# Samples' scores in short-lived banks, seven page slots, and half of w_out split during heads 2 to 5

## The chip, the cores and the metric

One core of one Trainium2 chip runs the whole kernel. The metric is the device time of one execution in microseconds; the time before is the median of three runs. A core has five engines with a queue each: TensorE (PE; its weight loads are PEld), VectorE (DVE), ScalarE (ACT), GpSimd (POOL) and SyncE (SP, which issues most DMAs here). Each engine takes its instructions in the order in which they were written for it.

## The reference

One layer of a decoder on 1024 prompt tokens and 8 samples of 4 tokens, width 1024, all in fp32:

- `z = LN(x) @ w_in`, cut into q, k, v, forget logits and the state-space input u
- attention: 8 heads of 64, `softmax(q k^T / 8 + c_q - c_k) v` with c the running sum of the forget logs; the prompt is causal over itself; each sample attends to 512 cached positions (4 pages of 128 rows, found by a page table) and its own 4
- the state-space mixer, then a gated unit: `y * sigmoid(y @ w_glu + b_glu)`
- `h1 = LN1(alpha h + concat(att, ssm) @ w_out)`, and after it a feed-forward layer, a gated embedding and LN2

## The kernel before, in words

Every matmul of fp32 precision is made of three in a faster format: an operand is split into a rounded part (hi, made by ScalarE) and a residual (lo, a subtraction); `split` is the helper, and hi*hi + hi*lo + lo*hi are summed. So a weight costs a load of its raw values, a ScalarE cast and a VectorE subtraction before PE can use it.

The change lies in the stage between about 290 and 545 us. Work there has three strands. **Heads.** For head h, `loads(h)` brings queries and keys into four tiles (eight DMAs, 1.6 MB), `weights(h)` makes the scores and exponentials of eight blocks of 128 queries, and `values(h)` does twelve steps: PE transposes the exponentials (tile tw), ScalarE copies them out (pe), VectorE rounds them (ph), GpSimd takes the residual (pl), PE multiplies both with the values (po; L909, L910). After step 4 and step 12 a half of the output is summed (oh) and sent to `mixd`. Values come with 0.25 MB a head, outputs leave with 0.25 MB. Scores run four blocks ahead of values. **The gated unit** (`glu`) reads y (`load_y`), splits it into slots u, multiplies, applies tanh, and writes `mixd` rows 512 and up (mo). **Samples** (`sample`) work in two halves of four samples: 16 key pages of 128x512 (0.26 MB each) are transposed on PE (tk) and copied out by ScalarE and VectorE in turn, 16 small matmuls after every fourth page give the scores (ssm, L990); then softmax, then five value steps of eight matmuls each (L1035), the first four with four value pages each. Pages go through six slots; `page()` issues the next load.

Gated unit and samples are generators in a queue `bg`, traced in between by `fill(t)`: each step has a price, and fill lets steps be traced until their prices reach the budget. The prices sum to 22.2 (gated unit) and 44.6 (samples). The budgets before the last scores sum to 61: 20 before head 0, 0.35 a step in heads 0 to 3, 0.6 after. A planner then orders each engine's instructions by a timeline of its own; `tc.issue_after(newest(SP))` forbids it to put a DMA ahead of SP's newest one at that point.

**After the heads** `load_wo` loads and splits w_out, 128 rows at a time: rows 4 to 7 (for the mixer's half of the input) into a pool opened when the query tiles are closed, rows 0 to 3 after the heads' pool is closed. `half(i, 4)` and `half(i, 0)` multiply a tile of 128 tokens of `mixd` with the two halves of w_out; `load_mx` loads that tile. The first two tiles' mixer halves run as `ssm` beside the last eight steps of head 7. PSUM has eight banks: three for scores (s), two for transposes (t), one for po (o) and two (f) that gated unit and samples share.

Of the kernel before, what the change touches and what calls it, by code (L numbers as in the profile page):

```python
# [8 lines left out]
F32 = mybir.dt.float32  # L9
F32R = mybir.dt.float32r  # L10
# [59 lines left out]
def fox_s5_step(tc, a, o):  # L70
# [764 lines left out]
    msk = aq_.tile([128, 512], F32, name="msk", bufs=1)  # L835
    G.memset(msk[:, 0:384], 0.0)
    G.tensor_copy(msk[:, 384:512], cst[:, TRI:TRI + 128])
    ins_, vs_, rows = {}, {}, {}

    def loads(h):  # L840
        hs_ = slice(h * 64, h * 64 + 64)
        qa = aq_.tile([128, T], F32R, tag="qa", name="qa")
        qb = aq_.tile([68, T], F32R, tag="qb", name="qb")
        ka = aq_.tile([128, T], F32R, tag="ka", name="ka")
        kb = aq_.tile([68, T], F32R, tag="kb", name="kb")
# [41 lines left out]
    def values(h):  # L887
# [5 lines left out]
        for u in range(2):  # L893
# [35 lines left out]


    def sample(bp):
        def page():
            t = bp.tile([128, AW], F32, tag="pg", name="pg", bufs=6)
            i, z = todo.pop(0)
            if z == "cache_k":
                pvs[i] = SY.value_load(idr[0:1, i:i + 1], min_val=0, max_val=a["cache_k"].shape[1] - 1)
            pv = pvs[i] if z == "cache_k" else pvs.pop(i)
            SY.dma_start(out=t, in_=a[z][0][bass.DynSlice(pv, 1)].rearrange("n t h d -> (n t) (h d)"))
            pages.append(t)
# [20 lines left out]
        for h in range(H):  # L960
# [5 lines left out]
                for g in range(4) for b4 in range(4)]  # L966
        for _ in range(6 - 1):
            page()
        yield 0.0
        for half in range(2):  # L970
            sel = cst[0:64, SEL + half * 128:SEL + half * 128 + 128]
            ps = bank("ssm", "f")
            PE.matmul(ps, lhsT=sel, rhs=nc_[:, 0:512], start=True, stop=False, skip_group_check=True)
            for g in range(4):
                kT = slot(2 + g % 2, F32)[:, 0:2048].rearrange("p (a b c) -> p a b c", a=4, b=4)
                for b4 in range(4):
                    kp = pages.pop(0)
                    if todo:
                        page()
                    t = bank("tk", "f").rearrange("p (k c) -> p k c", k=4)  # L980
                    for hp_ in range(4):
                        PE.transpose(t[:, hp_], kp[:, hp_ * 128:hp_ * 128 + 128], ident)
                    if b4 % 2:
                        V.tensor_copy(kT[:, b4], t)
                    else:
                        S.copy(kT[:, b4], t)
                    yield 0.45
                for hp_ in range(4):
                    for b4 in reversed(range(4)):
                        PE.matmul(ps[b4 * 32:b4 * 32 + 32, g * 128:g * 128 + 128], lhsT=qbd[:, half * 4 + b4, hp_],  # L990
                                  rhs=kT[:, b4, hp_], start=False, stop=(g == 3 and hp_ == 3),
                                  tile_position=(0, b4 * 32), skip_group_check=True)
                yield 0.95
            pn = bank("ssn", "f")[:, 0:8]
# [46 lines left out]
            om = bp.tile([128, AW], F32, tag="om", name="om", bufs=1)  # L1041
# [12 lines left out]

    for n in range(2):
        gp.tile([128, NB], F32, tag="sg", name="sg", bufs=2)
    gp.tile([128, NT], F32, tag="mo", name="mo")

    def load_y(m):
        t = gp.tile([128, NB], F32, tag="yf", name="yf", bufs=4)  # L1060
        if m < 3:
# [7 lines left out]
    def glu():  # L1069
# [16 lines left out]
        for m in range(4):  # L1086
            hi, lo = (x[:, :, m % 2 * 128:m % 2 * 128 + 128] for x in w[m // 2])
            sg = gp.tile([128, NB], F32, tag="sg", name="sg", bufs=2)
            yf = ys[m]
# [15 lines left out]
            ts(V, sg, sg, 0.5, MUL, 0.5, ADD)  # L1105
            mo = gp.tile([128, NT], F32, tag="mo", name="mo")
            yv = yf.rearrange("p (l c) -> p c l", l=L)
# [3 lines left out]
            SY.dma_start(out=mixd[AW + 128 * m:AW + 128 * m + 128], in_=mo)  # L1111
        gctx.close()

# [11 lines left out]
    bp = pool("smp", 2, stack=smctx)  # L1125
    ap_ = pool("att", 2, stack=actx)
    bg += [glu(), sample(bp)]
    lsum = ap_.tile([128, H, 12], F32, name="lsum", bufs=1)
    fill(1e-3)
    vload(0)  # L1130
    for i in range(4):
        steps(1)
        fill(5)
        if i == 1:
            loads(1)
    for h in range(H - 1):
# [18 lines left out]
    wo = {}  # L1155

    def load_wo(k, p, q, e=V):
        hi, lo = (p.tile([128, D], F32R, name=f"wo{n}{k}") for n in "hl")
        raw = q.tile([128, D], F32, tag="raw" if q is wp else "z", name="rawo", bufs=2 if q is wp else 3)
        SY.dma_start(out=raw, in_=a["w_out"][0][k * 128:(k + 1) * 128])  # L1160
        split(raw, hi, lo, e)
        wo[k] = hi, lo

    for k in range(4, 8):
        load_wo(k, woa, wp, V)
    mixv = mixd.rearrange("(k p) t -> p k t", p=128)
    dv = "p (c n) -> p c n"
    mxs, pss, order = {}, {}, [0, 1, 2, 3, 4, 5, 8, 6, 7]

    def load_mx(i):  # L1170
        mx = wp.tile([128, KD, 128], F32, tag="raw", name="mx", bufs=2)
        t0, r = tiles[i]
        SY.dma_start(out=mx[:, 4:8, :r], in_=mixv[:, 4:8, t0:t0 + r])
        return mx, [wp.tile([128, KD, 128], F32R, tag=t, name=t, bufs=2) for t in ("whi", "wlo")]

    def half(i, k0):
        t0, r = tiles[i]
        if k0:
            mxs[i] = load_mx(i)
            pss[i] = [bank("pso", t) for t in ("ss", "so")[order.index(i) % 2]]  # L1180
# [55 lines left out]
    for k in range(4):  # L1236
        load_wo(k, wop, op, V)
        next(ssm, None)
        fill(.5)
# [5 lines left out]

    ub = {(kh, 0): [h1p.tile([128, 4, HN], F32R, name=f"u{n}{kh}") for n in "hl"] for kh in range(2)}
    pend = []
# [520 lines left out]
```

## Time and profile before

| | before |
|---|---|
| median of 3 runs | 1450.24 us (1448.77 to 1460.35) |
| profiled execution | 1455.53 us, span 1453.8 us |
| PE busy | 1367.5 us, 94% |
| PE weight loads | 1267.7 us, 87% |
| VectorE | 981.4 us, 68% |
| ScalarE | 635.3 us, 44% |
| GpSimd | 676.2 us, 47% |
| mean granted clock of PE | 0.973 of full speed |

The profile shows one execution. Busy time counts instructions alone, and a busy PE at the lower clock counts like one at full speed. Windows give, for a stretch, the busy time of each engine, the granted clock and what the DMA engines did. The list of waits names what an engine's idle time ended on. A line of a helper (L82 for every addition or product of two tiles, L157 for the cast of `split`) stands for many places, so tiles tell more than lines. SP's rows show when a DMA was issued, not when it landed.

### The profile page before, as it was taken

The numbers are of one execution on the slowest core, as the hardware profiler recorded it, in microseconds if no ns is written. First come the engines' busy times: TensorE is split into PE (matmuls) and PEld (weight loads), VectorE is DVE, ScalarE is ACT, GpSimd is POOL, SyncE is SP. The second block draws the span as 40 slices with busy tenths as digits, with TensorE's granted clock in tenths as the row PEclk, the third lists the DMA queues.
The fourth block names the chain that finished last, engine by engine and source line by source line (L and its number), as shares of the span: only waits on it lengthen the run. The fifth ranks groups of instructions, "written<-read, shape, count | busy, mean of one in ns | idle before, by whom it ended". The sixth has DMA issues, their size and how long they took to land. (4 is left out here: it accounts for less than half of the span.)

```text
span 1453.8 us, 26634 instructions
## 1 busy us (share of the span) xinstructions
PE 1367.5 (94%) x10045; PEld 1267.7 (87%) x10045; DVE 981.4 (68%) x1579; ACT 635.3 (44%) x1188; POOL 676.2 (47%) x639
## 2 busy tenths in 40 slices
PE   6997999978979789999999999999999999999896
PEld 5887899877857558789999999999999999999796
DVE  8549599747977836568846555554555888888567
ACT  4422444446766624443325445454466344434212
POOL 4313012026656600028845443344347787777845
PEclk8999999989999989999999999999999999999898
DMA  7564255596876573323234444434467344556922
GB/s 280 175 131 109 77 152 137 159 250 180 204 183 170 140 224 108 91 66 93 78 104 128 147 162 163 132 128 149 149 227 260 115 128 162 163 163 171 181 67 102
DMA packets 209193, 218.38 MB, mean 150 GB/s; under 512 B 43977, under 2 KB 166473, under 8 KB 209065
## 3 DMA queue, kind: packets, MB, share of 16 engines
q1 hardware_dynamic: 197288, 178.02, 42.8%
q0 software_dynamic: 11776, 38.67, 8.3%
q8 instruction: 79, 1.29, 0.4%
q14 instruction: 50, 0.40, 0.1%
HBM read 143.59 MB, written 66.55 MB: 145 GB/s over the span
## 5 line engine op out<-in xcount | busy, mean ns | idle before, releaser
L1408 PE MATMUL pd<-x,a 128*128 128x264 f32 x1344 | 173.9, 289 | 10.0 <-ACT a L157 3.8
L1408 PEld LDWEIGHTS pd<-x,a 128*128 128x128 f32 x1344 | 169.4, 192 | 11.9 <-POOL a L82 4.2
L82 DVE TENSOR_TENSOR pacc<-pd,pacc 128x528 f32<-128x528 f32 x180 | 122.0, 701 | 66.1 <-PE pd L1408 60.4
L157 ACT CAST a<-s 128x256 fp32r<-128x256 f32 (+1 forms) x176 | 82.2, 485 | 180.4 <-PE pd L1408 75.1
L82 DVE TENSOR_TENSOR wlo<-raw,whi 128x1024 fp32r<-128x1024 f32 x68 | 103.8, 1527 | 46.1 <-ACT whi L157 33.8
L82 POOL TENSOR_TENSOR pl<-pe,ph 128x512 fp32r<-128x512 f32 (+1 forms) x96 | 104.6, 1100 | 61.7 <-DVE ph L905 35.6
L1408 PE MATMUL pb<-th,a 128*128 128x264 f32 x768 | 132.3, 284 | 0.0
L82 POOL TENSOR_TENSOR a<-s,a 128x256 fp32r<-128x256 f32 x112 | 105.8, 1002 | 55.3 <-ACT a L157 55.2
L82 POOL TENSOR_TENSOR s<-raw 128x256 f32<-128x256 f32 (+1 forms) x72 | 77.9, 1132 | 88.2 <-DVE a L82 65.9
L1408 PE MATMUL pd<-x,whi 128*128 128x264 f32 x672 | 109.1, 284 | 0.6 <-DVE pacc L82 0.6
L1408 PEld LDWEIGHTS pb<-th,a 128*128 128x128 f32 x768 | 109.2, 189 | 0.0
L82 DVE TENSOR_TENSOR x<-x 128x1056 fp32r<-128x1056 f32 (+2 forms) x68 | 95.3, 1433 | 7.2 <-ACT x L1429 6.3
L183 PE MATMUL mmc<-hhi,whi 128*128 128x352 f32 x288 | 94.7, 329 | 0.0
L183 PE MATMUL mmc<-hhi,wlo 128*128 128x352 f32 x288 | 94.4, 328 | 0.0
L1408 PEld LDWEIGHTS pd<-x,whi 128*128 128x128 f32 x672 | 93.4, 188 | 0.8 <-DVE pacc L82 0.8
L183 PE MATMUL mmc<-hlo,whi 128*128 128x352 f32 x288 | 93.8, 326 | 0.0
L82 POOL TENSOR_TENSOR rs<-rs,mh 128x1 f32<-128x1 f32 (+1 forms) x27 | 19.5, 731 | 158.4 <-DVE rs L86 156.1
L82 DVE TENSOR_TENSOR a<-s,a 128x512 fp32r<-128x512 f32 x64 | 47.5, 746 | 47.1 <-ACT a L157 42.8
L157 ACT CAST whi<-raw 128x1024 fp32r<-128x1024 f32 x48 | 50.5, 1052 | 63.4 <-PE pa L1408 27.0
L1408 PE MATMUL pb<-tl,a 128*128 128x264 f32 x384 | 78.1, 285 | 0.0
L882 ACT ACTIVATE row<-ss,nm 128x384 f32<-128x384 f32 (+4 forms) x96 | 55.6, 585 | 34.3 <-DVE nm L878 33.1
L905 DVE CAST ph<-pe 128x512 fp32r<-128x512 f32 (+1 forms) x96 | 61.2, 650 | 10.5 <-PE po L909 4.6
(470 smaller groups left out, 3948.8 us busy)
## 6 DMA issues: line engine op xcount, KB each, us to landing
x<-gd SPq DMA_DIRECT2D x53, 528.0 KB
raw<-in_w_up_dram SPq DMA_DIRECT2D x32, 512.0 KB
raw<-in_w_down_dram SPq DMA_DIRECT2D x120, 128.0 KB
gd<-e POOLq DMA_DIRECT2D x14, 1056.0 KB, 7.4
gd<-c POOLq DMA_DIRECT2D x14, 792.0 KB, 5.4
pg<-in_cache_k_dram SPq DMA_DIRECT2D x32, 256.0 KB
pg<-in_cache_v_dram SPq DMA_DIRECT2D x32, 256.0 KB
pacc<-pacc POOLq DMA_DIRECT2D x24, 264.0 KB, 6.6
```

The source lines that it names most:

```text
L82: e.tensor_tensor(out, x, y, op=op)
L157: S.copy(hi, x)
L183: PE.matmul(out, lhsT=wt[:, k], rhs=xt[:, k, c0:c0 + n], start=(k == 0 and i == 0), stop=(k == nk - 1 and i == 2))
L882: S.activation(out=pr_[:, c * n:(c + 1) * n], in_=ps, func=AF.Exp, scale=-1.0, bias=nm[:, i:i + 1], accum_out=lsum[:, h, i + 4 * c:i + 4 * ...
L905: V.tensor_copy(ph, pe)
L1408: PE.matmul(ps[:, p, :PC], lhsT=wt[:, k], rhs=xt[:, k, p * PC:(p + 1) * PC], start=(start and k == 0 and j == 0), stop=(k == n - 1 and j = ...
```

## The change

A head's queries and keys now live in two tiles of 128x2112 each instead of four of 128x1024; there are four such tiles for two heads, and later they hold the projection's result (`ub`), which before had a pool of its own opened after the heads. The gated unit's tiles become eight fixed slots g0 to g7, and w_out rows 4 to 7 (hi and lo) take the same slots later; these rows are loaded and split at the start of heads 2, 3, 4 and 5, behind SP's newest DMA, and the first two mix tiles are loaded at head 6. A sample half's scores are made in four banks, one for every four pages, each copied to SBUF (p) at once. Pages have seven slots; om uses one of them. The last page of a half's value phase is issued one step later. Budgets are 0.5 a step in heads 0 to 3 and 0.7 after, 72 before the last scores. The mask, rl and rlt move to other tiles, and oh has one slot instead of two.

```diff
@@ -824 @@
-    qctx, actx, h1bctx, h1ctx, smctx, gctx = (ExitStack() for _ in range(6))
+    actx, h1bctx, h1ctx, smctx, woctx = (ExitStack() for _ in range(5))
     h1x = pool("h1x", stack=h1ctx, side="right")
-    aq_ = pool("attq", 2, stack=qctx, side="right")
-    gp = pool("glu", stack=gctx, side="right")
+    h1p = pool("h1", stack=h1ctx, side="right")
+    gp = pool("glu", stack=woctx, side="right")
+    def hslot(j):
+        return h1p.tile([128, 4 * HN], F32R, tag=f"h{j}", name=f"h{j}")
+    def gslot(j, shape, d=F32):
+        return gp.tile(shape, d, tag=f"g{j}", name=f"g{j}")
+    for j in range(8):
+        gslot(j, [128, L * CB if j < 6 else NT if j == 6 else D])
...
     def loads(h):
-        qa = aq_.tile([128, T], F32R, tag="qa", name="qa")
...
+        qt, kt = (hslot(h % 2 * 2 + j) for j in range(2))
+        qa, qb, ka, kb = qt[:, 0:T], qt[0:68, T:2 * T], kt[:, 0:T], kt[0:68, T:2 * T]
@@ -911 @@
-            oh = ap_.tile([64, 512], F32, tag="oh", name="oh", bufs=2)
+            oh = ap_.tile([64, 512], F32, tag="oh", name="oh", bufs=1)
@@ -928 @@
+    NPG = 7
     def sample(bp):
         def page():
-            t = bp.tile([128, AW], F32, tag="pg", name="pg", bufs=6)
+            t = bp.tile([128, AW], F32, tag="pg", name="pg", bufs=NPG)
@@ -964 @@
-        for _ in range(6 - 1):
+        for _ in range(NPG - 1):
             page()
...
-            ps = bank("ssm", "f")
-            PE.matmul(ps, lhsT=sel, rhs=nc_[:, 0:512], start=True, stop=False, skip_group_check=True)
@@ -985 @@
+                gs_ = slice(g * 128, g * 128 + 128)
+                ps = bank("ssm", "f")[:, 0:128]
+                PE.matmul(ps, lhsT=sel, rhs=nc_[:, gs_], start=True, stop=False, skip_group_check=True)
                 for hp_ in range(4):
                     for b4 in reversed(range(4)):
-                        PE.matmul(ps[b4 * 32:b4 * 32 + 32, g * 128:g * 128 + 128], lhsT=qbd[:, half * 4 + b4, hp_],
+                        PE.matmul(ps[b4 * 32:b4 * 32 + 32], lhsT=qbd[:, half * 4 + b4, hp_],
...
+                V.tensor_copy(p[:, gs_], ps)
@@ -1006 @@
-            ts(V, p[:, 0:512], ps, cq1, ADD)
+            ts(V, p[:, 0:512], p[:, 0:512], cq1, ADD)
@@ -1034 @@
-                for _ in range(4):
+                if g == 3:
+                    om = bp.tile([128, AW], F32, tag="pg", name="om", bufs=NPG)
+                for _ in range((4, 4, 4, 3, 0)[g]):
                     if todo:
                         page()
...
+            if todo:
+                page()
@@ -1124 @@
+    msk = ap_.tile([128, 512], F32, name="msk", bufs=1)
...
+    def load_wo(k, q, e=V):
+        if k > 3:
+            hi, lo = (gslot(2 * k - 8 + j, [128, D], F32R) for j in range(2))
+        else:
+            hi, lo = (wop.tile([128, D], F32R, name=f"wo{n}{k}") for n in "hl")
+        raw = q.tile([128, D], F32, tag="raw" if q is wp else "z", name="rawo", bufs=2 if q is wp else 3)
+        with ExitStack() as st1:
+            if k > 3:
+                st1.enter_context(tc.issue_after(newest(mybir.EngineType.SP)))
+            SY.dma_start(out=raw, in_=a["w_out"][0][k * 128:(k + 1) * 128])
+        split(raw, hi, lo, e)
+        wo[k] = hi, lo
...
     for h in range(H - 1):
+        if 2 <= h < 6:
+            load_wo(h + 2, wp, V)
+        elif h == 6:
+            mxs.update((i, load_mx(i)) for i in range(2))
         for j, _ in enumerate(values(h)):
             if j < 4 or j % 2:
                 steps(1)
-            fill(.35 if h < 4 else .6)
+            fill(.5 if h < 4 else .7)
@@ -1146 @@
-        fill(.6)
+        fill(.7)
     steps(1)
-    qctx.close()
-    h1p = pool("h1", stack=h1ctx, side="right")
-    woctx = ExitStack()
-    woa = pool("woa", stack=woctx, side="right")
...
-    for k in range(4, 8):
-        load_wo(k, woa, wp, V)
@@ -1215 @@
-    rl = ap_.tile([128, H, 8], F32, name="rl", bufs=1)
+    rl = ap_.tile([128, 512], F32, tag="pe", name="rl", bufs=4)[:, 0:8 * H].rearrange("p (h i) -> p h i", h=H)
...
-    rlt = ap_.tile([64, 128], F32, name="rlt", bufs=1)
+    rlt = ap_.tile([128, 512], F32, tag="pe", name="rlt", bufs=4)[0:64, 0:128]
@@ -1243 @@
-    ub = {(kh, 0): [h1p.tile([128, 4, HN], F32R, name=f"u{n}{kh}") for n in "hl"] for kh in range(2)}
+    ub = {(kh, 0): [hslot(2 * kh + j).rearrange("p (k n) -> p k n", k=4) for j in range(2)] for kh in range(2)}
```

## Rows read from the trace of the kernel before

**Rows 1.** windows: stretch, length, busy us (count) PE PEld DVE ACT POOL, PEclk, DMA

```profile
300.00:314.00 14.00, 6.41 (x31) 5.05 (x29) 4.26 (x5) 5.25 (x7) 1.22 (x1) 0.77 1.08 224
...
364.00:403.00 39.00, 37.29 (x352) 31.64 (x351) 35.47 (x79) 30.67 (x84) 27.30 (x26) 1.00 0.89 206
...
416.00:442.00 26.00, 20.03 (x113) 11.73 (x112) 15.34 (x34) 12.66 (x36) 12.49 (x13) 0.87 0.85 227
...
453.00:489.00 36.00, 33.99 (x299) 28.64 (x297) 30.89 (x72) 28.18 (x77) 26.09 (x25) 1.00 0.56 138
...
489.00:518.00 29.00, 22.04 (x161) 15.81 (x162) 20.99 (x32) 13.71 (x27) 11.19 (x9) 0.88 0.54 157
...
518.00:544.00 26.00, 21.85 (x96) 14.07 (x95) 6.79 (x8) 4.19 (x4) 0.00 (x0) 0.87 0.85 263
...
544.00:590.00 46.00, 46.00 (x220) 37.61 (x219) 25.85 (x55) 19.09 (x40) 2.26 (x4) 1.00 0.36 98
```

**Rows 2.** the list of waits of PE, 290 to 600: us in total, times, longest

```profile
PE po L1035 <- DMA pg<-in_cache_v_dram: 5.7, 3, 3.2
...
PE ss L872 <- DMA kb<-kkd: 5.1, 1, 5.1
...
PE pso L1196 <- ACT woh L157: 4.1, 1, 4.1
...
PE tpp L1020 <- DVE u L86: 3.1, 1, 3.1
...
PE tk L982 <- ACT u L986: 0.7, 1, 0.7
...
PE tk L982 <- DVE u L984: 0.7, 3, 0.3
```

**Rows 3.** the timeline of SP, 280 to 600: start, length, issues of DMAs

```profile
284.14 0.33 SPq L1160 DMA_DIRECT2D rawo<-in_w_out_dram  x1
...
345.77 0.47 SPq L916 DMA_DIRECT2D mixd<-oh  x1
...
426.56 0.96 SPq L938 DMA_DIRECT2D pg<-in_cache_v_dram  x2
...
520.04 2.07 SPq L938 DMA_DIRECT2D pg<-in_cache_v_dram  x4
...
522.22 1.32 SPq L1160 DMA_DIRECT2D rawo<-in_w_out_dram  x3
```

**Rows 4.** groups of instructions by shape, 310 to 560: busy us, mean ns | idle before

```profile
L157 ACT CAST woh<-rawo 128x1024 fp32r<-128x1024 f32 x8 | 8.3, 1054 | 20.6 <-DMA rawo<-in_w_out_dram 20.6
...
L82 DVE TENSOR_TENSOR wol<-rawo,woh 128x1024 fp32r<-128x1024 f32 x8 | 10.9, 1368 | 14.0 <-ACT woh L157 13.9
...
L905 DVE CAST ph<-pe 128x128 fp32r<-128x128 f32 x16 | 4.9, 308 | 1.4 <-PE po L909 1.4
...
L82 POOL TENSOR_TENSOR pl<-pe,ph 128x512 fp32r<-128x512 f32 x48 | 66.5, 1393 | 39.4 <-DVE ph L905 26.7 <-PE po L910 8.7 <-PE po L909 1.6
```

**Rows 5.** the timeline of PE: value pages, and the projection's restart

```profile
433.99 1.93 PE L1035 MATMUL po<-pg,u 128*32 128x512 f32 x8 [3.22 <-DMA pg<-in_cache_v_dram]
...
530.03 2.08 PE L1196 MATMUL pso<-woh,whi 128*128 128x512 f32 x4 [4.15 <-ACT woh L157]
...
535.31 1.47 PE L1196 MATMUL pso<-woh,whi 128*128 128x512 f32 x4
...
541.38 1.06 PE L1035 MATMUL po<-pg,u 128*32 128x512 f32 x8
```

**Rows 6.** the timeline of DVE, 338 to 341 and 363 to 370

```profile
339.40 0.68 DVE L82 TENSOR_TENSOR oh<-po,ol 64x512 f32<-64x512 f32 x1
...
365.91 1.11 DVE L905 CAST ph<-pe 128x512 fp32r<-128x512 f32 x1
...
369.47 0.41 DVE L905 CAST ph<-pe 128x512 fp32r<-128x512 f32 x1
```

**Rows 7.** the tile mo: what its engine's idle time ended on

```profile
  DMA mixd<-mo: 0.4, 1
```

More of the change, by code (lines that the diff above doesn't have):

```diff
@@ L826, in fox_s5_step @@
     ptag[0] = "f"
-    qctx, actx, h1bctx, h1ctx, smctx, gctx = (ExitStack() for _ in range(6))
+    actx, h1bctx, h1ctx, smctx, woctx = (ExitStack() for _ in range(5))
     h1x = pool("h1x", stack=h1ctx, side="right")
-    aq_ = pool("attq", 2, stack=qctx, side="right")
-    gp = pool("glu", stack=gctx, side="right")
+    h1p = pool("h1", stack=h1ctx, side="right")
[6 more added lines that the diff above has]
+        gslot(j, [128, L * CB if j < 6 else NT if j == 6 else D])
     def slot(j, d=F32R):
         return (h1x, h1b)[j // 2].tile([128, 2 * L * CB], d, tag=f"u{j}", name="u", bufs=1)
-    msk = aq_.tile([128, 512], F32, name="msk", bufs=1)
-    G.memset(msk[:, 0:384], 0.0)
-    G.tensor_copy(msk[:, 384:512], cst[:, TRI:TRI + 128])
     ins_, vs_, rows = {}, {}, {}
@@ L841, in loads @@
         hs_ = slice(h * 64, h * 64 + 64)
-        qa = aq_.tile([128, T], F32R, tag="qa", name="qa")
-        qb = aq_.tile([68, T], F32R, tag="qb", name="qb")
-        ka = aq_.tile([128, T], F32R, tag="ka", name="ka")
-        kb = aq_.tile([68, T], F32R, tag="kb", name="kb")
+        qt, kt = (hslot(h % 2 * 2 + j) for j in range(2))
+        qa, qb, ka, kb = qt[:, 0:T], qt[0:68, T:2 * T], kt[:, 0:T], kt[0:68, T:2 * T]
         for j in range(2):
@@ L987, in sample @@
                     yield 0.45
+                gs_ = slice(g * 128, g * 128 + 128)
+                ps = bank("ssm", "f")[:, 0:128]
+                PE.matmul(ps, lhsT=sel, rhs=nc_[:, gs_], start=True, stop=False, skip_group_check=True)
                 for hp_ in range(4):
                     for b4 in reversed(range(4)):
-                        PE.matmul(ps[b4 * 32:b4 * 32 + 32, g * 128:g * 128 + 128], lhsT=qbd[:, half * 4 + b4, hp_],
-                                  rhs=kT[:, b4, hp_], start=False, stop=(g == 3 and hp_ == 3),
+                        PE.matmul(ps[b4 * 32:b4 * 32 + 32], lhsT=qbd[:, half * 4 + b4, hp_],
+                                  rhs=kT[:, b4, hp_], start=False, stop=(hp_ == 3),
                                   tile_position=(0, b4 * 32), skip_group_check=True)
+                V.tensor_copy(p[:, gs_], ps)
                 yield 0.95
@@ L1040, in sample @@
                 yield 1.9
-            om = bp.tile([128, AW], F32, tag="om", name="om", bufs=1)
             tt(V, om, po, om_c, MUL)
@@ L1053, in fox_s5_step @@
     ys = []
-    for n in range(2):
-        gp.tile([128, NB], F32, tag="sg", name="sg", bufs=2)
-    gp.tile([128, NT], F32, tag="mo", name="mo")
     def load_y(m):
-        t = gp.tile([128, NB], F32, tag="yf", name="yf", bufs=4)
+        t = gslot(m, [128, NB])
         if m < 3:
@@ L1087, in glu @@
             hi, lo = (x[:, :, m % 2 * 128:m % 2 * 128 + 128] for x in w[m // 2])
-            sg = gp.tile([128, NB], F32, tag="sg", name="sg", bufs=2)
+            sg = gslot(4 + m % 2, [128, NB])
             yf = ys[m]
@@ L1105, in glu @@
             ts(V, sg, sg, 0.5, MUL, 0.5, ADD)
-            mo = gp.tile([128, NT], F32, tag="mo", name="mo")
+            mo = gslot(6, [128, NT])
             yv = yf.rearrange("p (l c) -> p c l", l=L)
@@ L1111, in glu @@
             SY.dma_start(out=mixd[AW + 128 * m:AW + 128 * m + 128], in_=mo)
-        gctx.close()
     ahead = (x for h in range(H) for x in weights(h))
@@ L1126, in fox_s5_step @@
     ap_ = pool("att", 2, stack=actx)
+    msk = ap_.tile([128, 512], F32, name="msk", bufs=1)
+    G.memset(msk[:, 0:384], 0.0)
+    G.tensor_copy(msk[:, 384:512], cst[:, TRI:TRI + 128])
     bg += [glu(), sample(bp)]
@@ L1135, in fox_s5_step, with load_mx @@
             loads(1)
+    wo = {}
+    def load_wo(k, q, e=V):
[10 more added lines that the diff above has]
+        wo[k] = hi, lo
+    mixv = mixd.rearrange("(k p) t -> p k t", p=128)
+    mxs, pss, order = {}, {}, [0, 1, 2, 3, 4, 5, 8, 6, 7]
+    def load_mx(i):
+        mx = wp.tile([128, KD, 128], F32, tag="raw", name="mx", bufs=2)
+        t0, r = tiles[i]
+        SY.dma_start(out=mx[:, 4:8, :r], in_=mixv[:, 4:8, t0:t0 + r])
+        return mx, [wp.tile([128, KD, 128], F32R, tag=t, name=t, bufs=2) for t in ("whi", "wlo")]
     for h in range(H - 1):
+        if 2 <= h < 6:
+            load_wo(h + 2, wp, V)
+        elif h == 6:
+            mxs.update((i, load_mx(i)) for i in range(2))
         for j, _ in enumerate(values(h)):
@@ L1148, in fox_s5_step @@
         steps(1)
-        fill(.6)
+        fill(.7)
     steps(1)
-    qctx.close()
-    h1p = pool("h1", stack=h1ctx, side="right")
-    woctx = ExitStack()
-    woa = pool("woa", stack=woctx, side="right")
[L1155 to L1162, printed above, removed]
-    for k in range(4, 8):
-        load_wo(k, woa, wp, V)
-    mixv = mixd.rearrange("(k p) t -> p k t", p=128)
-    dv = "p (c n) -> p c n"
[L1168 to L1174, printed above, removed]
+    dv = "p (c n) -> p c n"
     def half(i, k0):
@@ L1178, in half @@
         if k0:
-            mxs[i] = load_mx(i)
+            if i not in mxs:
+                mxs[i] = load_mx(i)
             pss[i] = [bank("pso", t) for t in ("ss", "so")[order.index(i) % 2]]
@@ L1236, in fox_s5_step @@
     for k in range(4):
-        load_wo(k, wop, op, V)
+        load_wo(k, op, V)
         next(ssm, None)
```

## The prediction

> **What bounds the kernel now.** I read the page first: TensorE (PE) is busy for 94% of the span, so only idle or half-speed PE time can be won. The windows come next [rows 1]. From 544 us PE is busy for all of 46 us, and all that follows this stage simply starts later or earlier with it. The change touches what lies before: heads, gated unit, samples and the first row tiles of the projection. There the windows show four different limits. From 300 to 314 us PE is busy 6.4 of 14 us while the DMA share is over 1: it waits for the first query and key tiles, 5.1 us in one piece [rows 2]. In the two stretches in which the samples' key pages are transposed beside the heads (364 to 403, 453 to 489), PE is busy 37.3 of 39 and 34.0 of 36 us: 1.7 and 2.0 us are all that any change can win there. Where the samples' value pages are used (416 to 442), it is busy 20.0 of 26 us at a mean clock of 0.87; three waits for value pages come to 5.7 us [rows 2]. At the end (489 to 544), 7.0 and 4.2 us are idle, and mean clocks of 0.88 and 0.87 cost 12% of 29 and 13% of 26 us, 6.9 us more: 18 us in all. That is the largest loss, and there the list of waits has single pieces: 3.1 us for the samples' softmax, 4.1 us for the rounded w_out.
>
> **The change, part by part.** Terms are microseconds against the profiled execution (1455.5, span 1453.8).
>
> *Start.* Two w_out rows (4 and 5) are loaded at 284 and 321 us today, the first shown in [rows 3], long before any head; the new order edge keeps them behind head 2. One load is 128 x 1024 fp32, 0.52 MB, 2.3 us at the 224 GB/s of 300 to 314 [rows 1]. What waits there is the first scores. It may have been absorbed before 300, so between 0 and -2.3; I take -1, since the share over 1 says that something is still queued.
>
> *Key pages.* Today one of two "f" banks holds a half's scores for the whole phase; then the transposes of one page wait for the copy of the page before. The waits put down to that are 0.7 and 0.7 us [rows 2]. The new form frees the bank after sixteen matmuls, for eight more VectorE copies of 128x128; the nearest copy of that shape took 0.31 us [rows 4], 2.5 us in all. The addition of cq stays two instructions, now from SBUF. Four small selections replace one of the same columns. The seventh slot and the faster pace fill gaps of the first heads too. Ends: -3.7 (all idle time of both stretches) and +2.5 (all copies on the path); I take -1, near the waits shown.
>
> *Value pages of the first half.* Direct waits 5.7 us, and two groups from 434 us on took 1.93 us each (one shown) where the group at 541 took 1.06 [rows 5], 1.7 us more: 7.4 us to win. With seven slots two of the next four pages are in flight when a step runs, not one. But the phase is also short of bandwidth: its stretch moves 227 GB/s at a share of 0.85, one head takes 2.1 MB for queries, keys, values and output, and this phase (some 16 page loads, 4.2 MB) now lies in heads 2 and 3, with w_out rows 4 and 5 (1 MB, 4.6 us at that rate) added. So -2.5, between -7.4 and 0.
>
> *Value pages of the second half.* Today they trail through the tail (L1035 at 541 us). The fill budgets sum to 72 units before the last scores instead of 61, of the 67 that gated unit and samples ask for: the work now ends in head 6. Its matmuls move, which costs PE nothing; its waits come along. Only ten pages are left to load then, with one head's loads beside them. Between 0 and +7.4 (the first half's loss); I take +2.
>
> *Tail.* With no samples left, with w_out rows 4 to 7 split and the first two mix tiles loaded in head 6, head 7's second half has the first eight steps of the projection beside it. PE no longer waits for the softmax (3.1), and SP's w_out loads no longer stand behind value pages (520 to 522 us [rows 3]). What stays: rows 0 to 3 can only land in the tiles that the heads leave, so the 4.1 us wait stays, and so does the slow restart after it, 12 matmuls in the 5.3 us from 530.0 to 535.3 [rows 5] where 46 us of full clock hold 220 instructions [rows 1], 0.21 each: 2.8 us. That is 6.9, and I add 1.1 as less work is left to cover the loads. 18 - 8 = 10: -10, between -14 (only the 4.1 stay) and -3 (only the softmax wait goes).
>
> *Splits during heads 2 to 5.* Each is one ScalarE cast of 1.05 and one VectorE subtraction of 1.37 us [rows 4]; four of each, 4.2 and 5.5 us. From 364 to 403 (two heads) VectorE idles 3.5 us [rows 1], 1.8 a head: one subtraction fits, with little over, and ScalarE idles 4.2 a head. +2, between 0 and +9.7 (both wholly on the path). The raw loads add an issue to SP ahead of pages, and their tile is free once the gated unit's weights or an earlier row are split. The gated unit's tiles they reuse are done at 350 us, before head 2.
>
> By a row, the GpSimd residual of 128x512 took 1.39 us on average [rows 4] and POOL is busy 27.3 of 39 us [rows 1]. The same VectorE cast of 128x512 took 1.11 and 0.41 us within 4 us [rows 6], so something shared lengthens it. The Trainium skill, "GPSIMD Engine Reference", section Key points, says that GpSimd shares its SBUF interfaces with VectorE and contends with VectorE instructions that have two SBUF inputs; the moved subtractions are of that kind, and the spread of the cast agrees with it without proving it. By it the sum would lose half of its gain (rival c); I keep +2, because POOL has idle time left.
>
> *One output slot for a head's half.* VectorE's sum must now wait until the last half's output has left. The one such single slot in the trace, mo, cost 0.4 us once [rows 7]. But SP issued an output at 345.8 us whose sum ended at 340.1 [rows 3, 6], 5.7 us late behind other issues, and VectorE holds the next head's work behind it. +1, between 0 and +6.
>
> *At nothing:* mask, reciprocals and om in other tiles (no new instruction; hidden behind loads and other buffers of the same ring), query and key tiles merged (the same eight loads a head).
>
> Sum: -1 - 1 - 2.5 + 2 - 10 + 2 + 1 = **-9.5**, to 1446.0 of the profiled execution. That execution lies 0.4% above the median of 1450.24, so 1440.7, say 1441. The lowest ends sum to -27.4, the highest to +22.7. A measurement of this kernel tells 1% (14.5 us) from no change.
>
> **Rivals.** *(a) The waits vanish:* the seventh slot cures both value phases and the tail packs: -1 - 3.7 - 7.4 + 0 - 12 + 2 = -22, 1428. For: the waits are few and the extra page lies just where PE stands. Against: bandwidth as above.
>
> *(b) The DMA engines set the pace:* the same bytes must land before the tail whatever the order; heads 1 to 3, at 0.5 a step, ask for more pages than the 206 GB/s at share 0.89 carried from 364 to 403, plus two w_out rows. Then PE waits for pages in heads 2 to 6 what it saves at the end: -10 and twice -1 against no gain in the first value phase, 4.6 us for the two w_out rows in it, and 7.4 us in the second: 0, 1450. For: the share; against: 453 to 489 ran at 0.56, so there is room later.
>
> *(c) VectorE blocks POOL:* four subtractions of 1.37 us lengthen POOL's residuals one for one, and the last projection of each head waits: -9.5 + 5.5 = -4, 1446. The rule above would give this. Against: 11.7 of 39 us of POOL are idle.
>
> *(d) Slower: ScalarE stands behind w_out.* ScalarE is in order; if its four casts come up before their rows land, exponentials and evacuations of the head queue behind, and PE after them. The price: two value pages issued from 426.6 to 427.5 us let PE go only at 434.0 [rows 3, 5], 6.5 us; a w_out row is twice a page. Four such waits are 26 us, against -9.5: +16.5, 1467. It decides if the casts stand less than 6.5 us behind their loads. Against: SP has nothing to hold these loads back for 12 steps.
>
> *(e) Not what it says:* the loads keep their order and the pace does not change what the planner makes; 0, 1450.
>
> **Chances.** Forecast 0.53, spread from -3 to -19, a third of it beyond 1%; (a) 0.15; (b) 0.12; (c) 0.05; (d) 0.13; (e) 0.02. Faster by over 1%: 0.18 + 0.15 = 0.33. Slower: 0.13. Within: 0.54. Range: 1424 takes in (a) with 4 us to spare; at the upper side 1457 takes in (b), (c) and the forecast's upper terms and leaves (d) out.
>
> **What would show it.** In the profile after: no L1035 after head 7's scores and no softmax wait in the tail; w_out casts of rows 4 to 7 inside heads 2 to 5, without idle time of ScalarE ahead of them (with it, (d)); value-page waits of PE near 5 us in heads 2 and 3 (over 12: (b); under 1: (a)); no VectorE idle time ahead of oh that a DMA ends; PE at full clock some 9 us earlier than 544. The forecast is wrong if the tail keeps 14 us or more of loss, or if heads 1 to 6 grow by more than what the tail gives.

## The result: slower by 1.4%

The changed kernel took 1472.6 us (median of 4 runs, 1471.5 to 1473.6) beside 1453.5 for the kernel before in the same session: ratio 1.0138, 95% interval 1.0108 to 1.0168. The forecast was 1441, with a range from 1424 to 1457; the result lies outside, on the other side. Its profiled execution took 1471.7 us with a span of 1470.0 us, 16.2 more than the profiled span of before.

Where the time went is read head by head. These are windows of the kernel after, cut where a head's last output was summed (heads 1 to 7, then the projection): stretch, length, busy us (count) of PE, PEld, DVE, ACT, POOL, then PEclk and DMA.

```profile
365.40:387.20 21.80, 21.23 (x208) 18.30 (x212) 18.13 (x46) 16.84 (x49) 13.36 (x13) 1.00 0.84 215
387.20:412.10 24.90, 20.89 (x161) 16.09 (x149) 18.89 (x42) 13.79 (x37) 12.61 (x13) 0.86 0.58 141
412.10:439.10 27.00, 23.88 (x147) 16.94 (x149) 16.70 (x45) 16.88 (x49) 14.99 (x15) 0.87 0.91 259
439.10:466.40 27.30, 23.41 (x216) 19.55 (x209) 19.14 (x43) 15.42 (x41) 13.87 (x14) 0.87 0.71 185
466.40:492.60 26.20, 21.58 (x173) 15.60 (x173) 20.69 (x46) 17.10 (x45) 13.85 (x14) 0.94 0.58 137
492.60:515.80 23.20, 21.14 (x134) 14.52 (x131) 15.30 (x37) 14.25 (x41) 11.80 (x11) 0.99 0.39 117
515.80:540.50 24.70, 16.67 (x80) 12.17 (x79) 11.71 (x17) 7.40 (x16) 11.06 (x11) 0.86 0.24 64
540.50:560.00 19.50, 17.00 (x57) 12.81 (x58) 6.64 (x8) 4.26 (x5) 0.00 (x0) 0.82 0.84 257
```

The same windows of the kernel before, heads 1 to 6 and the stretch behind the heads (head 7, 489 to 518, is in [rows 1]):

```profile
363.70:382.30 18.60, 17.83 (x168) 15.23 (x168) 16.76 (x38) 14.17 (x40) 12.64 (x12) 1.00 0.85 196
382.30:402.60 20.30, 19.33 (x179) 16.30 (x179) 18.61 (x41) 16.40 (x48) 14.63 (x14) 1.00 0.92 213
402.60:422.40 19.80, 16.93 (x134) 12.54 (x133) 17.91 (x40) 12.45 (x35) 12.81 (x14) 1.00 0.57 140
422.40:452.60 30.20, 25.28 (x142) 17.05 (x140) 17.92 (x42) 15.97 (x47) 13.83 (x14) 0.89 0.80 204
452.60:470.60 18.00, 17.82 (x170) 15.19 (x169) 16.44 (x39) 13.91 (x38) 13.90 (x14) 1.00 0.73 175
470.60:489.00 18.40, 16.57 (x133) 13.75 (x131) 14.85 (x36) 14.67 (x41) 12.45 (x13) 1.00 0.40 102
...
518.00:560.00 42.00, 37.85 (x169) 27.05 (x167) 16.21 (x28) 8.97 (x11) 1.10 (x2) 0.92 0.75 221
```

For each window, idle time of PE plus what the clock took (one minus PEclk, times the length). Heads 1 to 6 lose 0.8 + 1.0 + 2.9 + 8.2 + 0.2 + 1.8 = 14.9 us before and 0.6 + 7.5 + 6.6 + 7.4 + 6.2 + 2.3 = 30.6 after: **15.7 us of the 16.2 lie in these heads, 15.5 of them in heads 2 to 5, which got the splits.** From there to 560 us it is 17.9 before and 17.5 after: the tail's forecast gain of 10 did not come either.

What PE waits for in these heads is named by the list of waits, 290 to 600 us (total, times, longest; the lines that answer to [rows 2], and the new ones):

```profile
PE po L914 <- POOL pl L82: 5.5, 11, 1.3
...
PE tw L904 <- ACT pe L908: 5.4, 5, 2.5
PE ss L876 <- DMA h<-kkd: 5.2, 1, 5.2
PE po L1043 <- DMA pg<-in_cache_v_dram: 4.5, 4, 1.4
PE ss L876 <- ACT row L886: 3.8, 3, 3.2
PE po L913 <- DVE ph L909: 3.2, 1, 3.2
...
PE pso L1211 <- ACT woh L157: 2.3, 1, 2.3
...
PE tk L986 <- DVE u L988: 0.5, 1, 0.5
```

The value pages cost less than before (4.5, not 5.7). ScalarE's two lines have grown: in the same list of the kernel before, the waits for the copies (pe) are 1.9 us and those for the exponentials (row) 2.2. The waits for GpSimd's residuals were 3.9 there; they are 5.5 too in a kernel without splits in the heads (m2 below). One place where PE waits for ScalarE, head 4, on ScalarE's timeline (start, length, operation, idle before it and its releaser):

```profile
443.82 1.06 ACT L908 COPY pe<-tw 128x512 f32<-128x512 f32 x2
447.67 1.04 ACT L157 CAST g<-rawo 128x1024 fp32r<-128x1024 f32 x1 [2.78 <-DMA rawo<-in_w_out_dram]
448.62 0.68 ACT L886 ACTIVATE row<-ss,nm 128x512 f32<-128x512 f32 x1
```

SP had issued that row at 439.96, among the next head's queries and keys:

```profile
439.96 0.53 SPq L1156 DMA_DIRECT2D rawo<-in_w_out_dram  x1
440.54 0.46 SPq L854 DMA_DIRECT2D h<-kkd  x1
```

And PE, in the same microseconds, waits for the exponential that stands behind the cast:

```profile
445.60 0.60 PE L986 MATMUL tk<-cst,pg 128*128 128x128 f32 x4
449.45 1.01 PE L876 MATMUL ss<-h,h 68*128 68x384 f32 x2 [3.25 <-ACT row L886]
```

What it costs is more than those 3.25 us, as two windows show:

```profile
445.00:449.00 4.00, 1.20 (x12) 0.96 (x9) 1.61 (x5) 1.33 (x2) 1.33 (x2) 0.94 1.09 254
449.00:454.00 5.00, 4.34 (x39) 2.81 (x40) 2.62 (x4) 3.73 (x11) 0.00 (x0) 0.50 0.75 219
```

PE is busy 1.20 of 4 us; then its granted clock is 0.50, the lower level (1.2 GHz), for all of the next 5 us. Idle 2.8 and 0.7, clock 0.2 and 2.5: 6.2 us for one wait of 2.78 us on ScalarE. The Trainium skill, "TensorE: Matmul & The Clock Gate", section "HAM oscillation — how this bites in real kernels", describes how a kernel that waits between its matmuls goes on at the lower clock and so falls below its rate. The rows agree in kind: the clock of 0.50 comes right behind the gap.

### The profile page after: what moved, and what is told of

Its sections match the earlier page's. It is cut to its first block, busy times and chain, and to the rows that moved or that the text cites. A ratio compares the mean times of both kernels' runs of the same rounds, so it can differ in the third digit from the quotient of the medians.

```text
span 1470.0 us, 26664 instructions
## 1 busy us (share of the span) xinstructions
PE 1373.3 (93%) x10057; PEld 1272.1 (87%) x10057; DVE 980.1 (67%) x1587; ACT 633.8 (43%) x1188; POOL 678.5 (46%) x639
## 5 line engine op out<-in xcount | busy, mean ns | idle before, releaser
L1423 PEld LDWEIGHTS pd<-x,a 128*128 128x128 f32 x1344 | 167.4, 190 | 11.8 <-POOL a L82 4.3
L1423 PE MATMUL pa<-h,whi 128*128 128x264 f32 x512 | 85.8, 285 | 1.4 <-ACT c L1500 0.7
```

The costliest lines, as they stand in the source:

```text
L1423: PE.matmul(ps[:, p, :PC], lhsT=wt[:, k], rhs=xt[:, k, p * PC:(p + 1) * PC], start=(start and k == 0 and j == 0), stop=(k == n - 1 and j = ...
```

## The experiments

Theory D: ScalarE, in order, stands behind w_out rows that were issued in the same head. Rivals: the faster pace (P), the short banks (B). Times are medians; a ratio is to runs of the kernel before on the same chip, with its interval. A step of 0.01 in the ratio is 14.5 us. One execution lies up to 0.5% off its median, so traces are read for mechanisms and ratios for sizes.

**e1_pace**: old pace in the changed kernel.

```diff
-            fill(.5 if h < 4 else .7)
+            fill(.35 if h < 4 else .6)
...
-        fill(.7)
+        fill(.6)
```

> The kernel after the change with the old pace of the planner alone (.35 a step in heads 0 to 3, .6 later). Theory D (ScalarE, in order, stands behind w_out rows that were loaded in the same head, and behind the two mix tiles): the waits stay, so under 4 us are won of the 19 lost: 1468 to 1474. Rival P (the faster pace crowds heads 1 to 4 with sample work and page loads): 12 us or more are won, under 1461.

1464.4, 1.0089 (1.0058 to 1.0120): about 7 us won, between the theories. ScalarE's wait for rows had also changed, from 7.5 to 3.8 us: the edit moved the casts too.

**e2_late_split**: loads and splits of rows 4 to 7 and the loads of the mix tiles written after the heads, without the order edge.

```diff
-            if k > 3:
-                st1.enter_context(tc.issue_after(newest(mybir.EngineType.SP)))
...
-        if 2 <= h < 6:
-            load_wo(h + 2, wp, V)
-        elif h == 6:
-            mxs.update((i, load_mx(i)) for i in range(2))
...
+    for k in range(4, 8):
+        load_wo(k, wp, V)
```

> The kernel after the change with w_out rows 4 to 7 loaded and split after head 7's scores, as before the change, and the two mix tiles loaded there too; pace, short banks, seven slots and the one output slot stay. Theory D: 15 us or more are won back in the heads, less what the tail then loses again (its part of the change was worth about 8 us), so 1455 to 1462 in all. Rival P: the heads stay as slow and the tail loses its 8 us: 1474 to 1482.

1463.6, 1.0073 (1.0046 to 1.0100). It isn't what I meant: the planner pulled the casts forward to 319, 337, 372 and 387 us, and 3.8 us of waits for rows remain. Where a line stands in the code does not say when its work runs.

**e3_load_ahead**: raw rows loaded in heads 1 to 4, split still written in heads 2 to 5.

```diff
+    def load_raw(k):
+        raws[k] = wp.tile([128, D], F32, tag="raw", name="rawo", bufs=2)
+        with tc.issue_after(newest(mybir.EngineType.SP)):
+            SY.dma_start(out=raws[k], in_=a["w_out"][0][k * 128:(k + 1) * 128])
...
+        if 1 <= h < 5:
+            load_raw(h + 3)
```

> The kernel after the change with w_out rows 4 to 7 loaded in heads 1 to 4, each one head ahead of its split, which stays in heads 2 to 5: the same work and bytes, only the wait goes. Theory D: ScalarE has no idle time that w_out rows end (7.5 us of it now), and with the clock that falls behind such a wait 8 us or more are won: under 1465. Rival P: the bytes press in head 1 already; under 3 us either way: 1470 to 1476.

1468.6, 1.0119 (1.0088 to 1.0150): little won, and the wait isn't gone. ScalarE's list of waits in this kernel:

```profile
ACT g L157 <- DMA rawo<-in_w_out_dram: 7.5, 3, 3.6
```

Rows issued at 365.9, 387.4, 414.5 and 438.5 us were cast at 370.4, 395.3, 423.0 and 447.0: the planner put each cast a few us behind its load again. The experiment failed to take the wait away, so it decides nothing.

**e4_one_bank**: one bank for a half's scores, no copies.

```diff
+            ps = bank("ssm", "f")
...
-                ps = bank("ssm", "f")[:, 0:128]
...
-                V.tensor_copy(p[:, gs_], ps)
...
```

> The kernel after the change with one bank for the scores of a half again, as before the change, and no copies of scores. Under theory D and rival P the short banks are a small gain of some 1 us: 1472 to 1476. Theory B (the eight copies on VectorE and the alternation of banks cost time beside the splits): 4 us or more are won, under 1469.

1459.4, 1.0058 (1.0035 to 1.0081): over 11 us won, more than D allows. ScalarE's waits for rows fell to 4.0 here too, and value pages became the first line of PE's waits (12.1 us).

**f1_hold_cast**: loads as in the changed kernel, casts held behind ScalarE's newest instruction one head later.

```diff
+    def split_wo(k):
+        with tc.issue_after(newest(mybir.EngineType.Activation)):
+            split(raws.pop(k), *wo[k], V)
...
+        if 3 <= h < 7:
+            split_wo(h + 1)
```

> The kernel after the change with the loads of w_out rows 4 to 7 where they are (heads 2 to 5), but each row's cast and subtraction put behind ScalarE's newest instruction one head later (heads 3 to 6), so that the row has landed when ScalarE comes to it. Theory D (ScalarE stands behind rows that have not landed): the 7.5 us of ScalarE's waits on them go, and 8 us or more are won: under 1464. Theory B (the short-lived score banks let the key pages of the samples run ahead and crowd their heads; the one-bank run won 13 us): under 4 us, 1468 to 1473.

1458.7, 1.0028 (1.0007 to 1.0049): 16 us won by ratio. This is the test that e3 was to be. The casts start 18 to 24 us behind their loads. The groups of the casts by shape (busy us, mean ns | idle before), first of the kernel after:

```profile
L157 ACT CAST g<-rawo 128x1024 fp32r<-128x1024 f32 x4 | 4.2, 1050 | 7.5 <-DMA rawo<-in_w_out_dram 7.5
```

and of this one:

```profile
L157 ACT CAST g<-rawo 128x1024 fp32r<-128x1024 f32 x4 | 4.2, 1045 | 0.0
```

The same four casts in the heads; only the idle time ahead of them is gone. Its windows by head:

```profile
363.90:385.70 21.80, 21.23 (x208) 18.30 (x212) 18.13 (x46) 16.82 (x49) 13.35 (x13) 1.00 0.84 213
385.70:405.40 19.70, 18.48 (x161) 13.74 (x149) 17.69 (x41) 13.49 (x37) 12.44 (x13) 1.00 0.75 182
405.40:431.40 26.00, 22.05 (x148) 16.47 (x152) 18.36 (x43) 16.23 (x46) 13.74 (x13) 0.87 0.97 267
431.40:452.40 21.00, 21.00 (x208) 18.03 (x201) 19.02 (x43) 15.81 (x42) 12.85 (x13) 1.00 0.86 228
452.40:478.00 25.60, 22.19 (x185) 17.83 (x183) 19.31 (x48) 16.49 (x45) 15.71 (x15) 0.93 0.58 142
478.00:500.50 22.50, 19.88 (x128) 13.97 (x127) 15.54 (x38) 15.17 (x44) 10.60 (x11) 1.00 0.43 133
```

Head 4 holds 208 matmuls in 21.0 us without a gap, where 216 took 27.3 before. Loss in heads 1 to 6: 0.6 + 1.2 + 7.3 + 0 + 5.2 + 2.6 = 16.9 us, not 30.6. One wait of the same kind is left, in head 5: the first mix tile's cast is not held, ScalarE stands 6.40 us before it (until 468.47; 3.25 us in the changed kernel), and PE 2.56 us behind ScalarE (until 469.52).

**f2_true_late**: as e2, with the order edge kept, so that no row of 4 to 7 can come before head 7.

```diff
-        if 2 <= h < 6:
-            load_wo(h + 2, wp, V)
-        elif h == 6:
-            mxs.update((i, load_mx(i)) for i in range(2))
...
+    for k in range(4, 8):
+        load_wo(k, wp, V)
```

> The kernel after the change with w_out rows 4 to 7 loaded behind SP's newest DMA after the heads' first twelve steps of head 7, split there, and the mix tiles loaded there; pace, short banks and seven slots stay. In the run without the order edge the planner had pulled the splits into heads 0 to 2; here none can come before head 7. Theory D: the second key-page phase loses its 13 us of extra PE loss, the tail gives back some 4: 1459 to 1464. Theory B: the banks' cost stays, and the tail's loss comes on top: 1470 to 1478.

1453.5, 0.9995 (0.9980 to 1.0011): all of the loss is gone, more than either theory gave, with pace, short banks, seven slots and one output slot still there.

**f3_before_banks**: the kernel before with the short banks.

```diff
-            ps = bank("ssm", "f")
...
+                ps = bank("ssm", "f")[:, 0:128]
...
+                V.tensor_copy(p[:, gs_], ps)
...
```

> The kernel before the change with the short-lived score banks alone (four banks a half, each copied to SBUF). Theory D: without w_out rows in the heads there is nothing that the faster key pages collide with: within 3 us of before, 1449 to 1455. Theory B: the banks cost by themselves what undoing them won: 8 us or more, over 1459.

1462.5, 1.0062 (1.0041 to 1.0082): 9 us lost by the banks alone, as B said.

**f4_before_pace**: the kernel before with the faster pace.

```diff
-            fill(.35 if h < 4 else .6)
+            fill(.5 if h < 4 else .7)
...
-        fill(.6)
+        fill(.7)
```

> The kernel before the change with the faster pace alone (.5 a step in heads 0 to 3, .7 later). Theory D: within 4 us of before or faster, 1446 to 1455, since undoing the pace in the changed kernel won its 8 us by spreading the w_out waits. Rival P: slower by 8 us or more, over 1459.

1446.1, 0.9953 (0.9935 to 0.9971): a gain of 7 us; rival P has the wrong sign.

**g1_late_one_bank**: f2's diff and e4's, both:

```diff
+            ps = bank("ssm", "f")
...
+    for k in range(4, 8):
+        load_wo(k, wp, V)
```

> The kernel after the change with two parts undone: w_out rows 4 to 7 and the mix tiles after the heads, and one bank for a half's scores. Pace, seven slots, the shared tiles and the one output slot stay. If the costs found so far add (splits in the heads 19 us, short banks 9 us alone, pace -7 alone), 1441 to 1447, faster than both kernels. If the banks cost only where w_out rows are in the heads (theory D alone), 1451 to 1456.

1455.6, 1.0023 (1.0008 to 1.0038). Not additive: beside f2, undoing the banks wins nothing. But VectorE now stands behind an output that has not left (its list of waits):

```profile
DVE oh L82 <- DMA mixd<-oh: 6.5, 3, 3.2
```

**g2_hold_one_bank**: f1's diff and e4's, both:

```diff
+            ps = bank("ssm", "f")
...
+        if 3 <= h < 7:
+            split_wo(h + 1)
```

> The kernel after the change with one bank for a half's scores and with each w_out row cast one head after its load. If the two costs add, 1449 to 1452; beside the run with the late splits it says what a split within a head costs once ScalarE does not wait for its row: 0 to 4 us under theory D, 6 us or more if the work itself is what the heads have no room for.

1464.4, 1.0092 (1.0059 to 1.0126), against both numbers expected. No cast of rows 4 to 7 waits here; PE waits 11.9 us for value pages, 10.1 of them after 440 us. With one bank the samples end later and their last pages meet the tail's loads. So it can't price the splits.

**g3_banks_slow_keys**: f3 with each key page's step at 0.65.

```diff
-                    yield 0.45
+                    yield 0.65
...
```

> The kernel before the change with the short-lived banks, and each key page's step counted 0.65 instead of 0.45 by the planner's budget, so that fewer key pages go beside a head (16 a head with the banks alone, 12 before). If the banks cost because the key pages run ahead: back within 3 us of before, 1450 to 1456. If the copies of the scores on VectorE are the cost: no better than the banks alone, 1460 or more.

1459.4, 1.0043 (1.0025 to 1.0062): between the two. The windows of the transposes (tile tk, four a page; PE's count comes first), of the kernel before from 338 to 388 us,

```profile
338.00:366.00 28.00, 2.55 (x16) 1.67 (x16) 1.35 (x2) 1.20 (x2) 0.94 0.73 181
366.00:388.00 22.00, 4.93 (x32) 3.69 (x32) 2.03 (x3) 2.36 (x4) 1.00 0.88 207
```

and of this kernel:

```profile
338.00:366.00 28.00, 4.47 (x28) 3.22 (x28) 1.77 (x3) 2.20 (x4) 0.88 0.62 174
366.00:388.00 22.00, 3.81 (x24) 2.96 (x25) 2.32 (x4) 1.77 (x4) 1.00 0.74 181
```

By 388 us 13 pages have passed here, 12 in the kernel before and 16 with the banks at the old price: the pages run ahead by less, and the loss is less, 6.2 us for 9.0. That fits pages that run ahead, but the two intervals overlap, and so does a cost of the copies. Open.

**g4_pace_slots**: the kernel before with pace and seven slots.

```diff
-            t = bp.tile([128, AW], F32, tag="pg", name="pg", bufs=6)
+            t = bp.tile([128, AW], F32, tag="pg", name="pg", bufs=7)
...
+                    om = bp.tile([128, AW], F32, tag="pg", name="om", bufs=7)
...
-            om = bp.tile([128, AW], F32, tag="om", name="om", bufs=1)
...
-            fill(.35 if h < 4 else .6)
+            fill(.5 if h < 4 else .7)
```

> The kernel before the change with the faster pace and the seven load slots (om in the ring, a half's last page one step later), nothing else. The prediction put the seventh slot at -2.5 in the first value-page phase and +2 in the second: 1442 to 1447. If the extra page in flight only moves the wait to SP (it stood 14 us behind one page in the changed kernel): 1446 to 1450.

1441.4, 0.9920 (0.9894 to 0.9946): 11.6 us faster, the best kernel here; the slot adds some 5 us to the pace's 7, though the two intervals overlap a little. PE's wait for value pages is 3.2 us instead of 5.7.

**k1_one_out_slot**: g4 with one output slot.

```diff
-            oh = ap_.tile([64, 512], F32, tag="oh", name="oh", bufs=2)
+            oh = ap_.tile([64, 512], F32, tag="oh", name="oh", bufs=1)
...
```

> The kernel before the change with pace and seven slots (1441.4 measured) and the one output slot for a head's half. The prediction gave that slot +1 (0 to 6). If it is what separates this kernel from the changed one with late splits and one bank (VectorE waited 6.5 us there for an output to leave): 1447 to 1455. If not: 1440 to 1444.

1446.7, 0.9949 (0.9928 to 0.9970): some 4 us dearer than g4, between the two bands and nearer the upper; the intervals of the two kernels overlap. The wait is there:

```profile
DVE oh L82 <- DMA mixd<-oh: 4.9, 3, 2.7
```

**h3_free_loads**: g1 with the order edge taken from the loads and put on the casts (behind ScalarE's newest instruction, after the heads).

```diff
-                st1.enter_context(tc.issue_after(newest(mybir.EngineType.SP)))
...
+                st1.enter_context(tc.issue_after(newest(mybir.EngineType.Activation)))
...
```

> The kernel after the change with one bank, the splits of w_out rows 4 to 7 after the heads, held there behind ScalarE's newest instruction, and their loads free to go as early as their tiles are (as before the change, when rows 4 and 5 were loaded at 284 and 321 us). If the order edge on the loads is what keeps the late form at 1455.6: 1443 to 1449. If not: 1453 to 1458.

1447.3, 0.9965 (0.9942 to 0.9987): 8 us better than g1. SP's timeline shows what the edge did. Of g1, the first two of the four rows (the others follow at 494.25 and 497.52):

```profile
486.06 1.07 SPq L1155 DMA_DIRECT2D rawo<-in_w_out_dram  x2
```

and of h3, where two rows leave long before head 2, as in [rows 3]:

```profile
282.50 0.33 SPq L1153 DMA_DIRECT2D rawo<-in_w_out_dram  x1
319.30 0.36 SPq L1153 DMA_DIRECT2D rawo<-in_w_out_dram  x1
489.76 0.34 SPq L1153 DMA_DIRECT2D rawo<-in_w_out_dram  x1
491.14 0.54 SPq L1153 DMA_DIRECT2D rawo<-in_w_out_dram  x1
```

**k4_tiles_only**: the changed kernel with old pace, six slots, one bank, two output slots and f2's late splits.

```diff
-            oh = ap_.tile([64, 512], F32, tag="oh", name="oh", bufs=1)
+            oh = ap_.tile([64, 512], F32, tag="oh", name="oh", bufs=2)
...
-    NPG = 7
+    NPG = 6
...
-            fill(.5 if h < 4 else .7)
+            fill(.35 if h < 4 else .6)
...
```

> The kernel after the change with everything undone but the shared tiles (queries and keys, gated unit and w_out), the moved mask and the order edge on the w_out loads: old pace, six slots, one bank, two output slots, splits after the heads. The prediction costed the tiles at nothing: 1449 to 1455. If the tiles cost what is open: 1458 or more.

1457.8, 1.0022 (0.9999 to 1.0045): 3 us, at the edge of what can be told; the edge on the loads is in it.

**h2_hold_late_mix**: f1 without the early mix tiles.

```diff
-        elif h == 6:
-            mxs.update((i, load_mx(i)) for i in range(2))
```

> The kernel after the change with each w_out row cast one head after its load (1458.7 measured) and the first two mix tiles loaded after the heads, not at head 6. ScalarE's wait for them in head 6 (3.3 us in the changed kernel) goes. Theory D for these tiles too: 2 to 5 us won, 1453 to 1457. If the early tiles pay in the tail what they cost: 1457 to 1461.

1456.6, 1.0022 (1.0000 to 1.0045), f1 was 1.0028. The edit did not take the wait away. Nothing holds these loads back, and the planner issued the first at 463.50 us, beside 462.79 in f1; ScalarE still stands before its cast:

```profile
469.69 0.62 ACT L1205 CAST whi<-mx 128x512 fp32r<-128x512 f32 x1 [5.98 <-DMA mx<-mixd]
```

So this run does not say what the early mix tiles cost.

**m1_banks_in_best**: g4 with the short banks.

```diff
-            ps = bank("ssm", "f")
...
+                ps = bank("ssm", "f")[:, 0:128]
...
+                V.tensor_copy(p[:, gs_], ps)
...
```

> The kernel before the change with pace and seven slots (1441.4 measured) and the short-lived banks. If the banks cost by their own work (eight copies, eight small selections), 1448 to 1452. If their cost depends on what value pages and pace leave room for: within 3 us, 1438 to 1445.

1449.8, 0.9987 (0.9967 to 1.0007): 9.7 us dearer than g4, as alone.

**m2_only_split_undone**: h3 with the short banks, so the changed kernel with nothing undone but the splits, the mix tiles and the edge.

```diff
-            ps = bank("ssm", "f")
...
+                ps = bank("ssm", "f")[:, 0:128]
...
+                V.tensor_copy(p[:, gs_], ps)
...
```

> The kernel after the change with only the splits of w_out rows 4 to 7 and the mix tiles put back after the heads, their loads free to go early (1447.3 with one bank). If the short banks cost by their own work: 1454 to 1458. If not: 1443 to 1449, faster than before the change.

1449.7, 0.9990 (0.9967 to 1.0013). Beside h3 the banks cost 3.6 us, less than the intervals can tell.

A chain of single steps from before to after, in us from the ratios: pace and slots -11.6 (g4), one output slot +4.2 (k1), shared tiles +2.3 (h3, whose late casts are held as well), short banks +3.6 (m2), splits and mix tiles in the heads, with the order edge on the rows' loads, +21.5: +20.0. Each middle step has an uncertainty of some 4 us; the first and the last stand far outside it.

## Why the prediction was wrong, step by step

**Splits during heads 2 to 5: the step that failed.** I priced the work (+2, at most +9.7) and left the wait to rival (d), with 0.13. The runs show the wait: +21.5 for the step (mix tiles and order edge included), of which holding the same casts (f1) takes 16 back; the rest is not told apart, but the wait for the first mix tile is in it. The rival's condition, casts less than 6.5 us behind their loads, came about in substance, though its figure was not the bound: 6.5, 6.2, 7.7 and 4.8 us lie between SP's issue of a row and its cast, and the cast after 6.2 us did not wait, while the other three began when the row landed. So did its price: 6.2 us for the wait shown above against 6.5. My reason against it was that nothing on SP holds these loads back. True, but beside the point: they left 0.5 to 2.3 us after the head began, among a head's queries and keys (the DMA share is 1.09 from 445 to 449 us), and the planner had set each cast right behind them. e3 shows that habit: loaded a head earlier, the casts went along.

**Tail, -10: not there in the changed kernel.** PE's wait for w_out fell from 4.1 to 2.3 and the samples were gone, as forecast, yet by the same reckoning 17.5 us stayed of 17.9. One cause is seen in the order of VectorE's timeline:

```profile
535.51 0.69 DVE L82 TENSOR_TENSOR mx<-mx,rb 128x512 f32<-128x512 f32 x1 [4.89 <-DMA mx<-mixd]
536.12 0.28 DVE L909 CAST ph<-pe 128x256 fp32r<-128x256 f32 x1
```

The first mix tile's product waits for the load of its attention half (SP issued it at 532.49), and head 7's last roundings wait behind it; PE stands for 3.25 us at 536.46; the list of which [rows 2] are taken has no such line. It is the same mistake of order on another engine. f1 keeps this wait (3.3 us), and its tail also loses 18.0 by the same reckoning. But the samples' early end did bring a gain, as long as the splits and mix tiles stood behind the heads. The same stretch in m2, from head 7 to 560 us:

```profile
494.90:519.10 24.20, 19.47 (x80) 13.86 (x81) 19.45 (x24) 12.43 (x23) 14.32 (x11) 0.86 0.57 156
519.10:560.00 40.90, 37.12 (x161) 28.47 (x160) 20.02 (x35) 12.80 (x20) 1.10 (x2) 1.00 0.58 176
```

That is 11.9 us, and 12.0 in g4, which has pace and slots alone. So some 6 of the 10 us came with the samples gone, and the failed step took them back: beside m2, whose heads 1 to 6 lose 11.8, the changed kernel loses 18.8 us more in these heads and 5.6 more behind them. What of the step costs the tail its gain is open.

**Value pages: right.** The first half's waits fell from 5.7 to 2.7 us (413.64 and 420.94), the second half's are 1.9, where I had taken -2.5 and +2. g4 shows the slot as a gain.

**Key pages, -1: wrong sign.** PE's waits for the copies fell from 1.4 to 0.5, as argued, and still the banks cost 9.0 and 9.7 us on the old tiles (f3, m1) and about 3.6 on the new ones. The eight copies' own time, 0.28 us each, is too little for it. Open.

**Start, -1: nothing.** The first scores wait 5.2 us (5.1 before). Of the two rows that I put before any head, the second leaves at 320.75 us, when the first scores of head 0 (314.03) have run, so at most the first could have been in their way. That the order edge keeps rows from landing early, which h3 prices at 8 us with late splits and one bank, I had counted as a gain. With short banks the same edit (f2 to m2) moved nothing that can be told, so its size depends on the rest.

**One output slot, +1:** +4.2, inside the ends given (0 to 6), too low.

**Rivals.** (b) fell: the lists of waits give value pages 4.5 us in all, not over 12. (c) did not happen at its price, though its mechanism can be seen. One of the four subtractions in the heads ran beside a residual of GpSimd:

```profile
425.75 1.22 DVE L82 TENSOR_TENSOR g<-rawo,g 128x1024 fp32r<-128x1024 f32 x1
425.98 2.14 POOL L82 TENSOR_TENSOR pl<-pe,ph 128x512 fp32r<-128x512 f32 x1 [3.37 <-DVE ph L909]
```

That residual took 2.14 us, where the median of the 48 of its shape is 1.28. In the kernel before, two of w_out's subtractions overlapped with four residuals, and two of these took 2.26 and 2.24 us. So these rows agree with the Trainium skill's rule on shared interfaces ("GPSIMD Engine Reference", Key points). But the other three subtractions in the heads met no work of GpSimd, so (c) cost less than 1 us here, not 5.5. The spread of VectorE's cast [rows 6] goes with GpSimd as well: in the kernel before, the twelve casts of 128x512 with no GpSimd work beside them took 0.41 to 0.43 us, and the 29 with GpSimd busy for at least half of their time 0.41 to 1.51, 0.90 on average.

**Sums.** The highest ends sum to +22.6, not +22.7. Rival (b)'s sum leaves out the +2 for the splits and the +1 for the slot, which would put it at 1453, and (a)'s leaves out the +1; the range takes them in all the same. Without tail and splits the forecast's other terms (start, pages, slot) sum to -1.5, and m2 measures -1.5; but m2 has a tail gain of some 6 us and larger losses than I gave in it, so that agrees by chance.

## What to carry to other kernels

Moving a weight's split into a busy stage costs little work and much order: an in-order engine that also evacuates for PE must not reach the cast before the row has landed. Load one stage ahead *and* hold the cast with an edge on its own engine; loading earlier alone let the planner pull the cast along (e3), and writing the code later alone did not move the work (e2, h2). Price such a wait by PE's idle time and the half clock behind it, here 6.2 us for 2.8 us on ScalarE.

## What was not expected of the hardware

One gap of 2.8 us in PE's work (1.20 of 4 us busy) was followed by 5 us at 1.2 GHz, although PE had 4.34 us of work in them. And a row of 0.5 MB issued among a head's loads took until 447.67 us, 7.7 us after its issue at 439.96, where 254 GB/s were moving (445 to 449 us): at that rate the row alone would take 2.1 us.
